# Seven-product feed-forward block: three of the seven products accumulate in PSUM onto three others, and the feature differences of the down projection are formed in the gate/up phase

## The chip, the cores and the metric

The kernel runs on one core of a Trainium2 chip, as one program. The metric is device time in microseconds (us), median of several executions. Beside the plain executions there is one profiled execution; every duration in this text comes from its trace. The engines are TensorE (PE, with its weight loads as PEld), VectorE (DVE), ScalarE (ACT), GpSimd (POOL) and SyncE (SP), which issues the transfers.

## The reference

A decoder trunk of two layers. Each layer mixes tokens in three ways (window attention, a state-space layer, latent attention), and then runs a gated feed-forward network, which is all that this change touches. Tokens: 1024. D_MODEL is 1024, D_FF is 2816.

```python
D_FF = ((8 * D_MODEL // 3 + 255) // 256) * 256
...
        h = rms_norm(x, ln2_g[l])
        x = x + (jax.nn.silu(h @ w_gate[l]) * (h @ w_up[l])) @ w_down[l]
    return rms_norm(x, final_g)
```

Everything is float32, so the kernel keeps about that precision: each operand of a matmul is split into a rounded part (hi) and the rest (lo), and three matmuls (hi by hi, hi by lo, lo by hi) stand for one.

## The kernel before

**Seven products for eight.** Activations lie with features on the partitions and tokens along the free axis, in two halves of 512 tokens (`HALF`). A feed-forward matmul is cut into 2 by 2 blocks of the weights and 2 by 2 of the activations (feature halves by token halves), and the four results are made of seven block products, as in Strassen's scheme, with Winograd's sums. The products are numbered 1 to 7. Each has a weight sum and an activation difference as operands, and the seven results are added into the four outputs, which the code calls (0,0), (0,1), (1,0), (1,1).

**One product.** `product` accumulates one product in one PSUM bank (tag `f`, 128 x 512 float32, 7 banks in the first layer and 8 in the second). For each slot of the contraction it issues three matmuls: L1621 (hi by hi), L1622 (hi weight, lo block), L1623 (lo weight, hi block). The weights come by DMA into `raw`; `halves` forms their sums `S` on DVE (L1563); `weight_block` and `split` make hi on ACT (cast, L242) and lo on POOL (L243) in tiles `wt`. The activation blocks are made by `combine` (a difference of two loaded tiles on DVE, L1606, in place) and `block` (hi by ACT, L1596; lo on DVE, L1597, or on POOL for products 5 and 7).

**Gate/up phase.** `ffn_begin` starts products 1 and 2 of the pairs 0 to 2 while the blocks of the other products are still being built; that stretch is called the head below. Then `ffn_pair` runs for the 11 pairs of 256 features. Each does seven products of four slots for gate and for up: 84 + 84 matmuls. `after` reads each finished product: ACT copies product 1, and DVE adds the others (L226) into the intermediate sums `u2`, `u3`, in tiles that are called B0 to B3, and into `gc`, `uc`. `finished` makes silu(gate) x up of one of the four results (tanh on ACT, then DVE at L235 and L226) and writes it to DRAM, into `actd`. A pair writes four results of 256 KB, 44 in a layer.

**Down stage.** `w_down` is walked in 15 windows: (d, p0, p1) is the output pair d with the feature pairs p0 to p1-1 as slots. A window runs the seven products over 2 to 4 slots. Where a window needs a feature pair for the first time, its four results are loaded from `actd` into B0 to B3, and its seven blocks are formed then, four of them by a difference. Eight windows bring pairs that are new (11 in all, hence 44 differences), seven bring none, the last among these. After each product DVE adds it, times one half, to one or two tiles of x (`TO`, at L235: x<-f,x), and products 1 and 6 also to a running sum `part` (tiles gs1, us1, gc, uc). In the windows without new pairs, but the last, product 5 goes by ACT (a copy `t`) and POOL (adds at L1839). The squares for the next norm are added on POOL (L1660).

**Order.** A scheduler orders the instructions of each engine from the program and its dependences. The order of the products is `ORDER` = 1, 2, 5, 6, 7, 3, 4, and `LAST` in the last window.

Of the kernel before, what the change touches and what calls it, by code (L numbers as in the profile page):

```python
# [22 lines left out]
HALF = 512  # L23
# [28 lines left out]
ORDER = (1, 2, 5, 6, 7, 3, 4)  # L52
LAST = (1, 2, 6, 7, 4, 5, 3)
BLOCKS = [[(b, k) for k in SLOTS for b in LAST[:2]], [(b, k) for k in SLOTS for b in LAST[2:]]]
BLOCKS[1:] = BLOCKS[1][:16], BLOCKS[1][16:]
TO = {1: ((0, 0),), 2: ((0, 0),), 5: ((0, 1), (1, 1)), 6: (), 7: ((1, 0), (1, 1)), 3: ((0, 1),), 4: ((1, 0),)}
# [3 lines left out]


# [154 lines left out]
class Trunk:  # L216
# [129 lines left out]
    def setup(self):  # L346
# [24 lines left out]
        self.actd = self.dp.tile([FT, 2, 128, HALF], F32, "actd")  # L371
# [1246 lines left out]
    def product(self, p, w, xs):  # L1618
        n = len(xs)
        for i, (k, (xh, xl)) in enumerate(xs):  # L1620
            self.T.matmul(p, w[0][:, k, :], xh, start=(i == 0), stop=False)  # L1621
            self.T.matmul(p, w[0][:, k, :], xl, start=False, stop=False)  # L1622
            self.last = self.T.matmul(p, w[1][:, k, :], xh, start=False, stop=(i == n - 1))  # L1623

    def after(self, b, p, tag, r):

        def new(n):
            if n[0] == "u":
                return self.ld.tile([128, HALF], F32, f"B{2 * int(n[1]) - 4 + (tag == 'u')}", 1)
            return self.fw.tile([128, HALF], F32, tag + n, 1)  # L1630
# [70 lines left out]
    def ffn_begin(self, l, pair, places):  # L1701
# [216 lines left out]
```

## Time and profile before

| what | us |
|---|---|
| median of three executions | 2389.26 (2388.66 to 2393.57) |
| profiled execution | 2391.46 |
| its span in the trace | 2389.5 |
| layer 0: head, gate/up, down | 101.1, 365.0, 254.5 |
| layer 1: head, gate/up, down | 100.1, 347.0, 254.5 |

The six stretches are 1422.2 us of the span. They were cut by hand at 503.9, 605, 970, 1224.5 in layer 0 and at 1669.9, 1770, 2117, 2371.5 in layer 1, where the first matmul of the head, the first of the steady pairs, the first of the down stage and its last stand. In layer 0 the gate/up stretch also holds tables for the next layer's state-space part, hence its greater length. Outside these stretches nothing is changed.

### The profile page before, as it was taken

What the parts mean: (1) busy time and instruction counts of PE and PEld (TensorE: products, weight loads), DVE (VectorE), ACT (ScalarE), POOL (GpSimd) and SP (SyncE); (2) the same over time, 40 slices, a digit from 0 to 9 for tenths busy, and PEclk for the clock granted to TensorE, in tenths of its full rate; (3) what the DMA queues carried; (4) which work ended last, traced back from release to release, by engine and by line L of the source; (5) the groups of instructions that cost most, each with busy time, mean ns of one, the idle gap of its engine ahead of it and who ended that gap; (6) DMA issues with size and microseconds to landing.
All of it is one profiled execution on the core that took longest, in us unless ns stands there. A gap on an engine that the chain in (4) does not pass through costs nothing. (4 is left out here: it accounts for less than half of the span.)

```text
span 2389.5 us, 31562 instructions
## 1 busy us (share of the span) xinstructions
PE 2233.2 (93%) x10460; PEld 1797.1 (75%) x10460; DVE 1754.5 (73%) x3079; ACT 996.6 (42%) x1992; POOL 1223.5 (51%) x1066
## 2 busy tenths in 40 slices
PE   7999889998999999899889998899899999999997
PEld 5688667876778878677668887687678888877776
DVE  7676975569876665998974578656886465689997
ACT  5254664543233333443333456544333333344334
POOL 1363653145565555677663354531555555557765
PEclk9899889998999999999989999899999999999999
DMA  6623343533332342432233232545252223243312
GB/s 214 178 77 74 100 115 127 178 100 88 117 109 84 97 129 79 127 112 88 81 119 81 65 107 65 153 127 155 88 165 88 85 74 93 67 128 101 108 60 81
DMA packets 263931, 255.85 MB, mean 107 GB/s; under 512 B 41450, under 2 KB 207193, under 8 KB 263769
## 3 DMA queue, kind: packets, MB, share of 16 engines
q1 hardware_dynamic: 263768, 253.84, 35.3%
q8 instruction: 83, 1.36, 0.2%
q14 instruction: 80, 0.65, 0.1%
HBM read 181.56 MB, written 65.92 MB: 104 GB/s over the span
## 5 line engine op out<-in xcount | busy, mean ns | idle before, releaser
L1621 PE MATMUL f<-b,wt 128*128 128x512 f32 x1848 | 740.8, 402 | 40.1 <-ACT wt L242 29.7
L1623 PE MATMUL f<-b,wt 128*128 128x512 f32 x1848 | 736.6, 402 | 21.3 <-POOL wt L243 20.5
L1622 PE MATMUL f<-b,wt 128*128 128x512 f32 x1848 | 736.6, 400 | 7.8 <-DVE b L1597 7.7
L243 POOL TENSOR_TENSOR wt<-raw,wt 128x512 fp32r<-128x512 f32 (+3 forms) x332 | 496.4, 1501 | 472.7 <-ACT wt L242 350.9
L1621 PEld LDWEIGHTS f<-b,wt 128*128 128x128 f32 x1848 | 354.3, 192 | 136.7 <-ACT wt L242 45.7
L1623 PEld LDWEIGHTS f<-b,wt 128*128 128x128 f32 x1848 | 354.4, 192 | 120.2 <-POOL wt L243 41.9
L243 POOL TENSOR_TENSOR wt<-S,wt 128x512 fp32r<-128x512 f32 (+2 forms) x222 | 300.5, 1355 | 272.9 <-ACT wt L242 269.6
L1622 PEld LDWEIGHTS f<-b,wt 128*128 128x128 f32 x1848 | 353.8, 191 | 91.3 <-DVE b L1597 13.7
L242 ACT CAST wt<-raw 128x512 fp32r<-128x512 f32 (+3 forms) x356 | 227.7, 646 | 305.4 <-PE f L1623 150.4
L242 ACT CAST wt<-S 128x512 fp32r<-128x512 f32 (+2 forms) x222 | 126.9, 573 | 247.6 <-DVE S L1563 158.6
L235 DVE SCALAR_TENSOR_TENSOR x<-f,x 128x512 f32<-128x512 f32 x216 | 141.6, 679 | 1.4 <-DVE x L235 0.5
L1596 ACT CAST b<-B 128x512 fp32r<-128x512 f32 x140 | 84.6, 618 | 136.6 <-DVE B L1606 83.7
L266 PE MATMUL mm<-b,wt 128*128 128x512 f32 x320 | 131.8, 412 | 7.3 <-DVE x L235 6.2
L267 PE MATMUL mm<-b,wt 128*128 128x512 f32 x320 | 128.2, 401 | 0.7 <-DVE b L235 0.7
L268 PE MATMUL mm<-b,wt 128*128 128x512 f32 x320 | 127.9, 400 | 0.0
L226 DVE TENSOR_TENSOR B<-B,f 128x512 f32<-128x512 f32 x176 | 119.2, 679 | 7.7 <-PE f L1623 4.1
L243 DVE TENSOR_TENSOR tl<-pt,th 128x512 fp32r<-128x512 f32 (+2 forms) x176 | 96.4, 553 | 38.2 <-ACT th L242 35.4
L1563 DVE TENSOR_TENSOR S<-raw,raw 128x512 f32<-128x512 f32 (+2 forms) x74 | 61.7, 836 | 72.5 <-DMA raw<-in_w_gate 38.2
L242 ACT CAST th<-pt 128x512 fp32r<-128x512 f32 (+2 forms) x176 | 82.9, 477 | 67.6 <-PE pt L1296 30.0
L1278 POOL TENSOR_SCALAR pr<-pr,den 128x128 f32<-128x128 f32 (+3 forms) x64 | 48.6, 763 | 120.4 <-DVE den L1277 117.5
L1597 DVE TENSOR_TENSOR b<-B,b 128x512 fp32r<-128x512 f32 x100 | 101.3, 1019 | 9.4 <-ACT b L1596 9.1
L1563 DVE TENSOR_TENSOR S<-raw,S 128x512 f32<-128x512 f32 (+2 forms) x74 | 69.5, 940 | 30.8 <-POOL wt L243 30.8
(440 smaller groups left out, 4152.8 us busy)
## 6 DMA issues: line engine op xcount, KB each, us to landing
raw<-in_w_gate SPq DMA_DIRECT2D x50, 512.0 KB, 3.8
raw<-in_w_up SPq DMA_DIRECT2D x50, 512.0 KB, 4.1
B<-actd SPq DMA_DIRECT2D x80, 256.0 KB, 2.9
raw<-in_w_out SPq DMA_DIRECT2D x32, 512.0 KB, 4.4
raw<-in_w_down SPq DMA_DIRECT2D x40, 384.0 KB, 3.2
x<-xe SPq DMA_DIRECT2D x48, 256.0 KB, 2.9
raw<-in_w_in SPq DMA_DIRECT2D x22, 512.0 KB, 4.4
actd<-gc SPq DMA_DIRECT2D x44, 256.0 KB, 2.1
```

Of the source, the lines that this page charges most:

```text
L226: self.V.tensor_tensor(out=out, in0=a, in1=b, op=op)
L235: self.V.scalar_tensor_tensor(out=out, in0=a, scalar=s, in1=b, op0=op0, op1=op1)
L242: self.A.copy(hi, src)
L243: (eng or self.V).tensor_tensor(out=lo, in0=src, in1=hi.bitcast(F32), op=ALU.subtract)
L266: self.T.matmul(ps, wh, xh, start=(i == 0), stop=False)
L267: self.T.matmul(ps, wh, xl, start=False, stop=False)
L268: self.T.matmul(ps, wl, xh, start=False, stop=(i == n - 1))
L1563: tt = lambda o, x, y, op: (self.G if b in self.gpre else self.V).tensor_tensor(out=o, in0=x, in1=y, op=op)
L1597: rest = lambda: (eng or self.V).tensor_tensor(out=t[1], in0=src, in1=t[0].bitcast(F32), op=ALU.subtract)
L1621: self.T.matmul(p, w[0][:, k, :], xh, start=(i == 0), stop=False)
L1622: self.T.matmul(p, w[0][:, k, :], xl, start=False, stop=False)
L1623: self.last = self.T.matmul(p, w[1][:, k, :], xh, start=False, stop=(i == n - 1))
```

## The change

Products 2, 3 and 4 no longer get a PSUM bank of their own. Product 2 is accumulated onto product 1, product 3 onto product 5, product 4 onto product 7, in the same bank, after the earlier one was read there. `ONTO` says which, `bank` hands out the bank, and the matmul starts without clearing it. The order becomes 1, 5, 2, 6, 7, 3, 4. So that the sums come out, the early products go to fewer outputs: `TO` lists five adds to x in a window where it listed eight. In the last window only product 2 is accumulated.

In the gate/up phase the (0,0) result is now finished straight from the two PSUM banks. All seven activation blocks of a pair (four of them differences) are formed there on DVE by `keep_blocks`, and all seven are written to `actd`, where four results were. In the down stage `stored` loads the seven, each into a tile of its own out of a rotation (x tiles, squares' tiles, B0 to B3), and `combine` is no longer called there. For the pairs 0 to 2 the (0,0) result is written in the head and loaded again.

```diff
-ORDER = (1, 2, 5, 6, 7, 3, 4)
-LAST = (1, 2, 6, 7, 4, 5, 3)
+ORDER = (1, 5, 2, 6, 7, 3, 4)
+ONTO = {2: 1, 3: 5, 4: 7}
+AHEAD, BUILT = (1, 2), (5, 6, 7, 3, 4)
+LAST = (1, 6, 2, 7, 4, 5, 3)
...
-TO = {1: ((0, 0),), 2: ((0, 0),), 5: ((0, 1), (1, 1)), 6: (), 7: ((1, 0), (1, 1)), 3: ((0, 1),), 4: ((1, 0),)}
+TO = {1: (), 2: ((0, 0),), 5: ((1, 1),), 6: (), 7: ((1, 1),), 3: ((0, 1),), 4: ((1, 0),)}
+TO_LAST = {**TO, 5: ((0, 1), (1, 1)), 7: ((1, 0), (1, 1))}
...
+        mm = lambda w, x, i: self.T.matmul(p, w, x, start=(i == 0 and not onto), stop=(i == 3 * n - 1), skip_group_check=onto)
...
         elif b == 2:
-            r[0, 0] = new("c")
-            self.tt(r[0, 0], r["s1"], p, ALU.add)
+            r[0, 0] = p
         elif b == 6:
-            r["u2"] = new("u2")
+            r["u2"], r[1, 1] = new("u2"), new("c")
             self.tt(r["u2"], r["s1"], p, ALU.add)
+            self.tt(r[1, 1], r["u2"], r[5], ALU.add)
         elif b == 7:
-            r["u3"], r[1, 1] = new("u3"), new("c")
-            self.tt(r["u3"], r["u2"], p, ALU.add)
-            self.tt(r["u2"], r["u2"], r[5], ALU.add)
-            self.tt(r[1, 1], r["u3"], r[5], ALU.add)
+            self.tt(r[1, 1], r[1, 1], p, ALU.add)
         elif b == 3:
-            self.tt(r["u2"], r["u2"], p, ALU.add)
-            r[0, 1] = r["u2"]
+            r[0, 1] = new("u3")
+            self.tt(r[0, 1], r["u2"], p, ALU.add)
         elif b == 4:
-            self.tt(r["u3"], r["u3"], p, ALU.add)
-            r[1, 0] = r["u3"]
+            r[1, 0] = r["u2"]
+            self.tt(r[1, 0], r["u2"], p, ALU.add)
+
+    def bank(self, b, r, ps, nf):
+
+        r[b] = r[ONTO[b]] if b in ONTO else ps.tile([128, HALF], F32, "f", nf)
+        return r[b]
...
+    def keep_blocks(self, pair, e, a):
+
+
+        def put(b, t):
+            self.dma(out=self.actd[pair, b], in_=t)
+        if e in ((0, 0), (1, 1)):
+            put(1 if e == (0, 0) else 3, a[e])
+        elif e == (0, 1):
+            self.tt(a[0, 0], a[0, 1], a[0, 0], ALU.subtract)
+            put(5, a[0, 0])
+            self.tt(a[0, 1], a[1, 1], a[0, 1], ALU.subtract)
+            put(7, a[0, 1])
+            self.tt(a[1, 1], a[1, 1], a[0, 0], ALU.subtract)
+            put(6, a[1, 1])
+        else:
+            put(2, a[1, 0])
+            self.tt(a[0, 0], a[1, 0], a[1, 1], ALU.subtract)
+            put(4, a[0, 0])
...
-            t = {}
-            for q in fresh:
-                t[q] = [self.ld.tile([128, HALF], F32, f"B{i}") if q else self.x_tile(i % 2, i // 2, False) for i in range(4)]
-                for i in range(4):
-                    self.dma(out=t[q][i], in_=self.actd[2 * q + i // 2, i % 2])
-            made = {}
+            def stored(b, q):
+
+                t = next(first if n < 2 else middle if n < ENDS else last)()
+                self.dma(out=t, in_=self.actd[q, b])
+                return self.block(b, q % 4, t, self.G if b in self.bsplit else None)
+            made, bank = {}, {}
...
-                p = ps.tile([128, HALF], F32, "f", nf)
-                self.product(p, next(ws), [(q - p0, self.blk[b][q % 4]) for q in range(p0, p1)])
+                onto = b in ONTO and not (end and b != 2)
+                p = bank[b] = bank[ONTO[b]] if onto else ps.tile([128, HALF], F32, "f", nf)
+                self.product(p, next(ws), [(q - p0, self.blk[b][q % 4]) for q in range(p0, p1)], onto)
...
-                for i, h in TO[b]:
+                for i, h in TO_LAST[b] if end else TO[b]:
```

The scheduler moves more than the diff shows. In the fences below, names are the program's, with buffer numbers. In layer 1's down stage, TensorE ran product 2 of window (3, 9, 11) right behind product 1, in a bank of its own (f_4852 after f_4848; the two wt tiles are their weights):

```order
L1621 MATMUL f_4848_21690<-b120_4813_21533,wt_4851_21695 128x512
L1622 MATMUL f_4848_21690<-b121_4814_21534,wt_4851_21695 128x512
L1623 MATMUL f_4848_21690<-b120_4813_21533,wt_4851_21695 128x512
L1621 MATMUL f_4852_21706<-b210_4801_21505,wt_4853_21707 128x512
L1622 MATMUL f_4852_21706<-b211_4802_21506,wt_4853_21707 128x512
L1623 MATMUL f_4852_21706<-b210_4801_21505,wt_4853_21707 128x512
```

In the changed kernel the same place reads as follows, from the last matmuls of product 4 of the window before (onto f_4673, that window's product 7) over products 6 (f_4690) and 7 (f_4692) of this one to product 2, which goes onto f_4681, where product 1 is.

```order
L1625 MATMUL f_4673_21438<-b421_4662_21372,wt_4676_21469 128x512
L1625 MATMUL f_4673_21438<-b420_4661_21371,wt_4676_21469 128x512
L1625 MATMUL f_4690_21534<-b620_4652_21353,wt_4691_21536 128x512
L1625 MATMUL f_4692_21547<-b710_4634_21317,wt_4693_21549 128x512
L1625 MATMUL f_4692_21547<-b711_4635_21318,wt_4693_21549 128x512
L1625 MATMUL f_4681_21494<-b210_4628_21305,wt_4689_21524 128x512
L1625 MATMUL f_4681_21494<-b211_4629_21306,wt_4689_21524 128x512
```

Between the end of product 1 and the start of product 2, and between 7 and 4, the order now holds some 20 matmuls of other products in the windows of two and three slots; product 4 of a window runs inside the window behind it.

On VectorE the down stage of before has, around window (1, 5, 8) of layer 1, the block differences (L1606), the lo parts (L1597), the adds of a product to x (L235) and to the running sum us1 (L226):

```order
L226 TENSOR_TENSOR us1_4462_19973<-us1_4462_19973,f_4585_20521 128x512
L235 SCALAR_TENSOR_TENSOR x2_0_4418_19871<-f_4585_20521,x2_0_4418_19871 128x512
L1597 TENSOR_TENSOR b211_4643_20782<-B2_4634_20752,b210_4642_20781 128x512
L1597 TENSOR_TENSOR b611_4652_20823<-B0_4632_20750,b610_4651_20822 128x512
L235 SCALAR_TENSOR_TENSOR x2_0_4418_19871<-f_4591_20544,x2_0_4418_19871 128x512
L1606 TENSOR_TENSOR B2_4634_20752<-B2_4634_20752,B0_4632_20750 128x512
L235 SCALAR_TENSOR_TENSOR x2_1_4419_19873<-f_4595_20563,x2_1_4419_19873 128x512
L235 SCALAR_TENSOR_TENSOR x3_1_4421_19877<-f_4595_20563,x3_1_4421_19877 128x512
```

The changed kernel has there, for the same window (products 1 and 2 in f_4556, product 6 in f_4565; f_4552 is products 7 and 4 of a window before):

```order
L230 TENSOR_TENSOR us1_4304_19831<-us1_4304_19831,f_4556_20933 128x512
L1601 TENSOR_TENSOR b401_4619_21275<-B0_4617_21272,b400_4618_21274 128x512
L239 SCALAR_TENSOR_TENSOR x1_0_4377_20175<-f_4552_20882,x1_0_4377_20175 128x512
L1567 TENSOR_TENSOR S_4597_21176<-raw_4590_21152,raw_4591_21154 128x384
L239 SCALAR_TENSOR_TENSOR x2_0_4254_19725<-f_4556_20933,x2_0_4254_19725 128x512
L230 TENSOR_TENSOR us1_4304_19831<-us1_4304_19831,f_4565_20982 128x512
L1567 TENSOR_TENSOR S_4576_21058<-S_4576_21058,raw_4572_21040 128x384
```

The differences are gone and each bank of two products has one add to x at its end. Counted over a whole layer, the adds x<-f,x go from 108 to 71, the 44 differences of the down stage to none (40 of them on B tiles), POOL's adds at L1839 from 12 to 6, and the 44 differences come back in the gate/up phase. The end of a pair there had adds of a product's bank and the finishing of a result, as here:

```order
L226 TENSOR_TENSOR B0_4203_18569<-B0_4203_18569,f_4216_18639 128x512
L235 SCALAR_TENSOR_TENSOR B0_4203_18569<-t_4220_18675,B0_4203_18569 128x512
L226 TENSOR_TENSOR B1_4206_18588<-B1_4206_18588,f_4218_18657 128x512
L226 TENSOR_TENSOR B0_4203_18569<-B0_4203_18569,B1_4206_18588 128x512
L226 TENSOR_TENSOR B2_4209_18607<-B2_4209_18607,f_4221_18680 128x512
```

DVE's order now has at such a place:

```order
L230 TENSOR_TENSOR B2_4165_19088<-gc_4154_19007,B2_4165_19088 128x512
L239 SCALAR_TENSOR_TENSOR B0_4153_19006<-t_4171_19150,B0_4153_19006 128x512
L230 TENSOR_TENSOR gc_4154_19007<-gc_4154_19007,gc_4149_18983 128x512
L230 TENSOR_TENSOR B1_4157_19027<-B1_4157_19027,f_4161_19049 128x512
L230 TENSOR_TENSOR B0_4153_19006<-B0_4153_19006,B1_4157_19027 128x512
L230 TENSOR_TENSOR gc_4149_18983<-B0_4153_19006,gc_4154_19007 128x512
```

Three of these rows (the first, third and last) are differences. In exchange a full pair has ten adds of a PSUM bank where it had fourteen, since product 2 needs none and products 6 and 7 need fewer. SP issues 77 writes to `actd` in a layer where it issued 44, and 77 loads from it (and 3 more in the gate/up phase) where it issued 44.

## Rows read from the trace of the kernel before

**Rows 1.** The page: busy time and share of the span, by engine.

```profile
PE 2233.2 (93%) x10460; PEld 1797.1 (75%) x10460; DVE 1754.5 (73%) x3079; ACT 996.6 (42%) x1992; POOL 1223.5 (51%) x1066
```

**Rows 2.** Busy time by stretch: head, gate/up, down of layer 0, then of layer 1.

```profile
core 0: us, PE busy (x) PEld busy (x) DVE busy (x) ACT busy (x) POOL busy (x), PEclk, DMA share, GB/s
503.90:605.00 101.10, 88.47 (x362) 68.22 (x361) 88.14 (x111) 36.68 (x63) 58.06 (x38) 0.92 0.30 91
605.00:970.00 365.00, 361.63 (x1597) 291.91 (x1596) 255.92 (x359) 115.56 (x203) 198.73 (x154) 0.99 0.33 102
970.00:1224.50 254.50, 230.75 (x926) 175.26 (x924) 235.13 (x297) 106.67 (x209) 186.54 (x143) 0.97 0.36 107
1669.90:1770.00 100.10, 88.92 (x363) 68.20 (x361) 83.72 (x104) 36.52 (x63) 58.21 (x38) 0.91 0.39 122
1770.00:2117.00 347.00, 347.00 (x1512) 283.73 (x1511) 216.47 (x291) 111.20 (x188) 181.41 (x130) 1.00 0.28 87
2117.00:2371.50 254.50, 232.95 (x929) 177.40 (x927) 228.14 (x297) 106.42 (x209) 180.44 (x140) 0.95 0.28 84
```

**Rows 3.** Waits of TensorE in layer 1's down stage: us, times, longest.

```profile
PE f L1621 <- ACT wt L242: 10.6, 11, 1.9
PE f L1623 <- POOL wt L243: 7.4, 10, 1.5
```

**Rows 4.** Waits of ScalarE in the same stretch.

```profile
ACT wt L242 <- DVE S L1563: 58.9, 22, 7.5
ACT b L1596 <- DVE B L1606: 42.4, 19, 5.8
ACT b L1596 <- DMA B<-actd: 26.2, 15, 3.9
```

**Rows 5.** Busy time in four short stretches of it; columns as in group 2.

```profile
2117.00:2132.20 15.20, 12.53 (x45) 8.82 (x44) 11.35 (x16) 6.66 (x15) 7.89 (x7) 0.89 0.58 189
2203.70:2221.70 18.00, 14.92 (x43) 9.80 (x42) 17.40 (x23) 8.17 (x17) 11.94 (x11) 0.72 0.46 131
...
2319.80:2334.20 14.40, 11.64 (x44) 7.27 (x43) 11.99 (x20) 7.32 (x16) 7.63 (x9) 1.00 0.10 30
2334.20:2357.00 22.80, 18.55 (x65) 13.75 (x64) 15.21 (x18) 8.16 (x17) 22.24 (x18) 0.85 0.06 18
```

**Rows 6.** VectorE by line and shape, same stage: busy us, mean ns, idle before.

```profile
L235 DVE SCALAR_TENSOR_TENSOR x<-f,x 128x512 f32<-128x512 f32 x107 | 70.1, 679 | 0.6
L1597 DVE TENSOR_TENSOR b<-B,b 128x512 fp32r<-128x512 f32 x50 | 50.1, 1009 | 5.4 <-ACT b L1596 5.3
L1606 DVE TENSOR_TENSOR B<-B,B 128x512 f32<-128x512 f32 x40 | 43.2, 1080 | 1.7 <-POOL b L1597 1.6
```

**Rows 7.** PE at line L1623 alone, 2117.05 to 2187.70 us; then VectorE's timeline.

```profile
2117.05:2187.70 70.65, 33.24 (x85) 16.57 (x84) 0.95 0.36 112
...
2199.14 0.68 DVE L226 TENSOR_TENSOR us<-us,f 128x512 f32<-128x512 f32 x1
```

**Rows 8.** POOL by line, layer 1's down stage.

```profile
L1839 POOL TENSOR_TENSOR x<-x,t 128x512 f32<-128x512 f32 x12 | 17.9, 1513 | 0.0
```

**Rows 9.** VectorE in layer 1's gate/up phase, by line, then one of its waits.

```profile
L226 DVE TENSOR_TENSOR B<-B,f 128x512 f32<-128x512 f32 x69 | 46.9, 680 | 0.4
L226 DVE TENSOR_TENSOR B<-B,B 128x512 f32<-128x512 f32 x17 | 18.2, 1072 | 0.3
...
DVE B L226 <- PE f L1623: 60.2, 16, 6.9
```

**Rows 10.** VectorE in layer 1's head (1669.9 to 1737 us), by line.

```profile
L226 DVE TENSOR_TENSOR gc<-gc,uc 128x512 f32<-128x512 f32 x3 | 5.1, 1690 | 0.1
L235 DVE SCALAR_TENSOR_TENSOR gc<-acc,gc 128x512 f32<-128x512 f32 x3 | 3.5, 1183 | 0.0
```

**Rows 11.** DMA issues on SP's queue: count, KB each, us from issue to landing.

```profile
B<-actd SPq DMA_DIRECT2D x80, 256.0 KB, 2.9
...
actd<-gc SPq DMA_DIRECT2D x44, 256.0 KB, 2.1
```

More of the change, by code (lines that the diff above doesn't have):

```diff
@@ L59 @@
            (2, 5, 8), (3, 6, 9), (0, 8, 11), (3, 9, 11), (1, 8, 11), (2, 8, 11)]
+ENDS = next(i for i, (d, a, b) in enumerate(WINDOWS) if b == WINDOWS[-1][2])
 def _bits12(v):
@@ L370, in setup @@
         self.xe = self.dp.tile([2, KT, 128, HALF], F32, "xe")
-        self.actd = self.dp.tile([FT, 2, 128, HALF], F32, "actd")
+        self.actd = self.dp.tile([FT // 2, 8, 128, HALF], F32, "actd")
         self.zd = [self.dp.tile([128, 8, 128], F32, f"zd{i}") for i in range(2)]
@@ L1629, in new @@
                 return self.ld.tile([128, HALF], F32, f"B{2 * int(n[1]) - 4 + (tag == 'u')}", 1)
-            return self.fw.tile([128, HALF], F32, tag + n, 1)
+            return self.fw.tile([128, HALF], F32, tag + n, 1 + (tag + n == "gc"))
         r[b] = p
@@ L1713, in ffn_begin, with finished @@
         self.begun[pair] = r
-        for b in ORDER[:2]:
+        for b in AHEAD:
             for m in range(2):
-                p = self.fps.tile([128, HALF], F32, "f", self.nf)
+                p = self.bank(b, r[m], self.fps, self.nf)
                 w = self.weight_block(b, raw[m][:, 4 * b - 4:4 * b])
-                self.product(p, w, [(k, self.blk[b][k]) for k in SLOTS])
+                self.product(p, w, [(k, self.blk[b][k]) for k in SLOTS], b in ONTO)
                 yield
                 self.after(b, p, "gu"[m], r[m])
-        self.finished(pair, (0, 0), r, self.sqp.tile([128, HALF], F32, "acc1", 1))
-    def finished(self, pair, e, r, t=None):
+        t = self.sqp.tile([128, HALF], F32, "acc1", 1)
+        self.finished(pair, (0, 0), r, t, t)
+        self.dma(out=self.actd[pair, 1], in_=t)
+    def finished(self, pair, e, r, t=None, out=None):
         g, u = r[0][e], r[1][e]
         t = self.fw.tile([128, HALF], F32, "t", 1) if t is None else t
+        out = g if out is None else out
         self.act(t, g, AF.Tanh, scale=0.5)
-        self.stt(g, t, 1.0, g, ALU.add, ALU.mult)
-        self.tt(g, g, u, ALU.mult)
-        self.dma(out=self.actd[2 * pair + e[0], e[1]], in_=g)
+        self.stt(out, t, 1.0, g, ALU.add, ALU.mult)
+        self.tt(out, out, u, ALU.mult)
+        return out
     def ffn_pair(self, l, pair):
@@ L1737, in ffn_pair @@
         r = self.begun.pop(pair, None)
-        order = ORDER[2:] if r else ORDER
+        order = BUILT if r else ORDER
+        a = {}
+        new = lambda: self.fw.tile([128, HALF], F32, "gc", 2)
+        if r:
+            a[0, 0] = new()
+            self.dma(out=a[0, 0], in_=self.actd[pair, 1])
         r = r or [{}, {}]
@@ L1742, in ffn_pair @@
             for m in range(2):
-                p = self.fps.tile([128, HALF], F32, "f", self.nf)
-                self.product(p, next(ws[m]), [(k, self.blk[b][k]) for k in SLOTS])
+                p = self.bank(b, r[m], self.fps, self.nf)
+                self.product(p, next(ws[m]), [(k, self.blk[b][k]) for k in SLOTS], b in ONTO)
                 yield
@@ L1747, in ffn_pair @@
             for e in DONE.get(b, ()):
-                self.finished(pair, e, r)
+                a[e] = self.finished(pair, e, r, None, new() if e == (0, 0) else None)
+                self.keep_blocks(pair, e, a)
+    def keep_blocks(self, pair, e, a):
[14 more added lines that the diff above has]
+            put(4, a[0, 0])
     def ffn(self, l, tp, side, other):
@@ L1774, in ffn @@
             self.late = []
-            for b in ORDER[2:]:
+            for b in BUILT:
                 for k in SLOTS:
@@ L1795, in ffn @@
         part = {}
+        spare = [lambda i=i: self.ld.tile([128, HALF], F32, f"B{i}", 1) for i in range(4)]
+        early = [lambda i=i: self.x_tile(i % 2, i // 2, False) for i in range(4)]
+        early += [lambda: self.sqp.tile([128, HALF], F32, "sq", 3)] * 3
+        early += [lambda h=h: self.sqp.tile([128, HALF], F32, f"acc{h}", 1) for h in range(2)]
+        first, middle, last = (itertools.cycle(x) for x in (early, early[4:] + spare, spare))
         def add(dst, src):
@@ L1820, in ffn @@
                     for b in ORDER:
[L1821 removed]
+                        made[b, q] = stored(b, q)
             for b in order:
```

15 lines of the change are left out of this document (7 added, 8 removed).

## The prediction

> **What bounds the kernel now.** I began with the page: TensorE is busy 93% of the span, VectorE 73% [rows 1]. That is an average over stages, so the next view is the table by stretch [rows 2]. In layer 1's gate/up phase PE is busy 347.00 of 347.00 us with 1512 matmuls, 229.5 ns each, at a granted clock of 1.00: nothing can be won there unless matmuls go, and the change takes none away. The two down stages have 926 and 929 matmuls in 254.5 us. At 229.5 ns they would take 212.5 and 213.2, so 42.0 and 41.3 us are time in which PE was kept waiting or was slowed. The heads have 362 and 363 matmuls in 101.1 and 100.1 us, 83.1 and 83.3 at that pace: 18.0 and 16.8 over. The most that any change to this block can win with the same matmuls is therefore 83.3 + 34.8 = 118 us.
>
> What keeps PE waiting in the down stage? By the waits it is weight tiles, the hi part from ACT (10.6 us) and the lo part from POOL (7.4) [rows 3]. Followed one step back, ACT itself waits 58.9 us for the weight sums S of VectorE, 42.4 us for the block differences at L1606, and 26.2 us for loads [rows 4]. So VectorE is late, and its busy time says why: 235.13 and 228.14 us, more than the 213 that PE needs [rows 2]. In the two gate/up phases VectorE is busy 255.92 of 365 and 216.47 of 347, 70% and 62%, and there 1597 and 1512 matmuls run at 228.6 and 229.5 ns: no excess at either share.
>
> The excess isn't spread evenly. Four short stretches hold 5.1 + 8.1 + 4.3 + 7.9 = 25.4 of layer 1's 41.3 us (length less PEld's count times 0.2295: 15.2 - 10.1, 18.0 - 9.9, 14.4 - 9.9 and so on, rounded) [rows 5]. In the second VectorE is busy 17.40 of 18.0 and the granted clock is 0.72. In the last POOL is busy 22.24 of 22.8: it, not VectorE, is the bound there.
>
> **The change, part by part.** *Adds to x.* 37 of 108 go per layer. One takes 0.679 us [rows 6]: 25.1 us less on VectorE.
>
> *Differences in the down stage.* 44 go per layer, 40 of them on B tiles at 1.080 us [rows 6]; I take these 40, 43.2 us, and leave the four on x tiles out. VectorE then has 235.1 - 68.3 = 166.8 and 228.1 - 68.3 = 159.8 us, 78 and 75% of PE's 213. It is no longer the bound of the stage.
>
> *POOL.* Six of twelve adds at L1839 go, 1.513 us each [rows 8]: 9.1 us of 186.5 and 180.4, so some 177 and 171 remain, 83 and 80% of 213. POOL is next.
>
> *ACT.* It makes as many copies and casts as before. Its 42.4 us of waits for differences fall away; the blocks wait for a load instead.
>
> *Transfers.* 77 loads from actd in a layer for 44, and 77 writes for 44, of 256 KB. A load landed 2.9 us after its issue, a write 2.1 us [rows 11]. The DMA share in the stages is 0.28 to 0.36 [rows 2]; loads that grow by 33 x 256 KB = 8.4 MB, over the 84 GB/s of 254.5 us = 21.4 MB, make about 0.39. The bounds are nothing (they are issued ahead into nine or more tiles) and, if each of the 33 more held up the blocks behind it by its 2.9 us, 96 us. I take nothing for the steady windows, because ACT's waits for loads cost PE little even now (26.2 us on ACT beside PE's waits for blocks too small to be among the rows), and keep a part of the high end in the third case below.
>
> *Gate/up phase.* A full pair gets four differences, two SBUF operands each, 1.072 us by the nearest row, and loses four adds of a bank, 0.680 us [rows 9]: 4.3 - 2.7 = 1.6 us more a pair, 13 us in eight pairs. VectorE had 216.5 of 347 and waits 60.2 us for PE there [rows 9], so PE does not notice: zero. Without that cover it would cost 13 us a layer. The two rows differ in one operand, a bank or a second SBUF tile. [...] The sum itself takes POOL's durations as they are.
>
> *The head.* The adds that make (0,0) go: six at about 0.68 us. gc<-gc,uc (5.1 us for three) and gc<-acc,gc (3.5) become operations on a bank, six at 0.68 [rows 9, 10]: 4.1 + 8.6 - 4.1 = 8.6 us a layer less on VectorE, which builds the blocks that PE waits for. The bounds of the gain are 0 and 8.6, since part of the excess is in ACT and weights; I take half, 4. A new wait: product 2 starts one product (12 matmuls, 2.8 us) after product 1's end and ACT must have copied it by then. Nothing in the rows prices it; it lies before the blocks are complete, and the half that I give away covers it.
>
> *Shared banks.* In a window of the down stage product 2 waits until product 1 has been read by VectorE, and 4 until 7 was. The order puts some 20 matmuls between, 20 x 0.2295 = 4.6 us. How late does VectorE read now? By 2187.70 us PE had loaded 84 weights of line L1623, 7 x (2 + 3 + 3 + 4), the first four windows. The fifth window's product 1 is the next 9 matmuls, about 2.1 us, so it ended near 2190.0; us<-us,f, which reads it, began at 2199.14 [rows 7]. That is 9 us, twice the slack. But VectorE was then over 90% busy; at 75 to 78% its queue should be short. Lower bound: no wait. Upper bound: 9.1 - 4.6 = 4.5 us in each of 28 waits a layer, 126 us. I take 3 us a layer, near the low end, since the nearest rows at such a load, the gate/up phases, show PE without excess, though reads there trail too. What would wait with it: matmuls of the other products queued behind on PE, then ACT and POOL for free weight tiles. On the other side, a window now holds four banks for seven, which lets PE run further ahead; I give that nothing.
>
> **The sum.** Of some 41.7 us of excess in a down stage, the POOL-bound stretch (7.9) keeps 6, as one of its adds (1.5) goes. Of the other 34, a share remains that I scale by VectorE's load: none at 70% (the gate/up phase), all at 109% (mean of 235.1 / 212.5 and 228.1 / 213.2), and 76.5% lies at (76.5 - 70) / 39 = 17%; I take a quarter, 8 us, for the starts of windows, which wait on transfers. With 3 for the banks 17 remain and 24.7 go, 49 us in two layers. With 4 us from each head it is 57 us. The profiled execution took 2391.5 us; 2391.5 - 57 = 2334.5. The median of the runs lies 2.2 below the profiled one, so the forecast is **2332 us**.
>
> **The rivals.** *First (forecast), 0.60:* as above; its own range is 2310 to 2358, that is, 11 us more or 13 us less won in each layer than I took.
>
> *Second, 0.17: PE runs through.* VectorE's release also frees POOL and ACT, and only 6 us of a down stage remain: 35.7 x 2 = 71, with the whole 8.6 us of both heads 88 us: 2391.5 - 88 - 2.2 = 2301. For it: the waits of ACT on VectorE (58.9 and 42.4) are far the largest in the stage. Against: POOL at 80% and more.
>
> *Third, 0.13: weights or transfers take over.* POOL's lo parts already make PE wait 7.4 us [rows 3], and it stays at 80 to 83%; 33 more loads stand in SP's queue among the weights' own. If three quarters of the excess stays under a new name, some 10 us a layer go and the head gives nothing: 2391.5 - 20 - 2.2 = 2369. For it: the last of the short stretches is POOL's already [rows 5].
>
> *Fourth, 0.10: slower, by the shared banks.* The reads stay as late as they are, because VectorE's queue is in a fixed order and holds lo parts that wait for blocks (5.3 us of such idle time, [rows 6]) ahead of a bank's read. With 28 waits a layer, the whole excess of 42 us is eaten at 42 / 28 = 1.5 us a wait, a lag of 6.1 us; beyond that the kernel is slower. At 2 us it is 56 us a layer against 42 won: 28 us more in both, 2389.3 + 28 - 8 = 2409. The 9 us of today speak for it, the fall of VectorE's load against it. [...]
>
> **How the numbers follow.** About 0.2%, 4.8 us, is what a measurement of this kernel can tell from no change. The range 2294 to 2378 holds the first case whole, about two thirds of the second and most of the third, some 8 in 10; above it lies the fourth. The first two and most of the third are faster: 0.86. The third's weak end, with a few small bank waits on top, gives no change: 0.04. Slower: 0.10.
>
> **What would show each step.** Right: the two down stages fall from 254.5 to about 230 us; VectorE there is near 160 to 167 us, with about 71 adds x<-f,x; ACT's wait for differences is gone; the last short stretch is still POOL's; gate/up phases stay within 2 us of 365 and 347; the heads lose about 4 us. Wrong: a line of PE waiting for VectorE's x or us, gs, gc at the start of a product, of over 40 us a layer (fourth case); PE waiting for POOL's wt or ACT's b behind loads, over 20 us a layer (third); a gate/up phase over 350 us in layer 1, which would mean that the differences there are not hidden; a head longer than before, which would be the copy of product 1.

## The result, and the profile after

| what | before | after |
|---|---|---|
| median, us | 2389.32 (2388.66 to 2393.57, 4 runs) | 2332.28 (2330.30 to 2337.12, 4 runs) |
| ratio | | 0.9761 (95%: 0.974 to 0.9781) |
| profiled execution's span | 2389.5 | 2328.6 |

The forecast of 2332 us was met, 57 us less than before. The terms behind it were not met one by one, so the result is worth taking apart. First the table by stretch of the changed kernel, in the order of [rows 2] and with the same columns (head, gate/up, down, of layer 0 and then of layer 1):

```profile
498.50:601.00 102.50, 86.94 (x362) 68.02 (x360) 89.32 (x112) 36.51 (x63) 57.16 (x38) 0.95 0.37 110
601.00:968.20 367.20, 363.01 (x1596) 292.44 (x1597) 269.96 (x352) 118.82 (x212) 205.55 (x155) 0.99 0.41 131
968.20:1190.20 222.00, 216.86 (x926) 173.75 (x926) 175.34 (x221) 102.97 (x196) 167.75 (x135) 0.99 0.44 139
1634.90:1734.70 99.80, 86.92 (x362) 68.22 (x361) 83.20 (x100) 36.41 (x63) 57.81 (x38) 0.95 0.45 143
1734.70:2086.30 351.60, 349.10 (x1513) 285.04 (x1512) 234.03 (x286) 114.34 (x196) 188.90 (x131) 1.00 0.36 116
2086.30:2310.80 224.50, 218.85 (x928) 176.18 (x926) 174.16 (x224) 105.81 (x200) 161.49 (x132) 0.98 0.38 120
```

The down stages lost 32.5 and 30.0 us, 62.5 together, where 49 were forecast. The heads changed by +1.4 and -0.3 where 8 were to be won, and the gate/up phases got longer by 2.2 and 4.6 where nothing was to change. In all that is 54.6 us (1422.2 down to 1367.6). The rest of the span's 60.9 lies outside these stretches, most of it ahead of the first head, which begins at 498.5 us for 503.9. TensorE's order up to there isn't quite that of before, since the scheduler moved some projections. But of the kernels below, five with before's order (it among them) begin the head at 500.1 to 506.0 us and nine with the order of the change at 498.5 to 509.8, so those 5 us are spread, not gain. The medians lie 57.0 us apart, 3.9 less than the two profiled spans.

The waits of TensorE in layer 1's down stage, answering to [rows 3], hold the new kind, a product waiting for the reader of the bank that it goes onto (the first two lines; us and x are the readers' outputs):

```profile
PE f L1625 <- ACT us L1874: 2.1, 1, 2.1
PE f L1625 <- DVE x L239: 2.0, 1, 2.0
PE f L1625 <- POOL wt L247: 1.3, 2, 0.9
PE f L1625 <- ACT wt L246: 0.3, 1, 0.3
```

They are 5.7 us where the two lines of [rows 3] held 18.0. ScalarE's waits in the same stretch, answering to [rows 4]:

```profile
ACT wt L246 <- PE f L1625: 37.6, 36, 3.1
ACT wt L246 <- DVE S L1567: 37.1, 18, 3.3
...
ACT b L1600 <- DMA acc<-actd: 4.4, 2, 2.4
ACT b L1600 <- DMA sq<-actd: 4.3, 4, 1.4
```

The 42.4 us for block differences are gone, and first comes a wait for TensorE: ACT is ahead and waits for weight tiles that PE still reads. For about as long (37.1 us) it waits for VectorE's weight sums. PE is now what holds ACT up in much of the stage.

To see where in the stage the time went, I cut it by count of matmuls into a start (the first 84), a middle (672) and an end (168). At 229.5 ns, the pace of the prediction, they need 19.3, 154.2 and 38.6 us. Layer 1 of the changed kernel, columns as above:

```profile
2086.30:2112.60 26.30, 22.95 (x86) 17.25 (x85) 25.64 (x36) 13.56 (x27) 18.58 (x14) 0.87 0.81 268
2112.60:2267.50 154.90, 154.90 (x674) 126.22 (x673) 114.05 (x147) 68.64 (x129) 110.23 (x93) 1.00 0.40 123
2267.50:2310.80 43.30, 41.00 (x172) 32.70 (x170) 34.48 (x42) 23.61 (x44) 32.68 (x26) 0.96 0.06 19
```

And the kernel before, cut the same way:

```profile
2117.10:2143.80 26.70, 22.79 (x85) 16.30 (x84) 22.84 (x33) 11.84 (x24) 13.71 (x11) 0.94 0.44 135
2143.80:2319.80 176.00, 165.37 (x674) 128.08 (x673) 164.22 (x207) 70.48 (x139) 129.43 (x99) 0.96 0.32 96
2319.80:2371.50 51.70, 44.69 (x172) 32.95 (x170) 40.97 (x58) 24.08 (x46) 37.30 (x32) 0.93 0.05 16
```

The middle went from 176.0 to 154.9 us, all that could be won there; the end from 51.7 to 43.3; the start hardly at all. Of the middle's 21.1 us, 10.6 were idle time of TensorE (176.00 less 165.37 busy). The other 10.5 are the same 674 matmuls done in 154.90 us of busy time for 165.37: before, the granted clock stood at 0.5 for 13.7 us of the middle (0.96 over the whole of it), and after it never did there (1.00). In the start, where 7.0 us over PE's need are left (26.3 - 19.3; 7.4 before), VectorE is busy 25.64 of 26.30 us.

### The profile page after: what moved, and what is told of

It reads as the page before. It is cut to its first block, busy times and chain, and to the rows that moved or that the text cites. A ratio compares the mean times of both kernels' runs of the same rounds, so it can differ in the third digit from the quotient of the medians.

```text
span 2328.6 us, 31600 instructions
## 1 busy us (share of the span) xinstructions
PE 2201.8 (95%) x10460; PEld 1792.4 (77%) x10460; DVE 1671.7 (72%) x2917; ACT 1000.7 (43%) x1992; POOL 1200.8 (52%) x1054
## 5 line engine op out<-in xcount | busy, mean ns | idle before, releaser
L1625 PE MATMUL f<-b,wt 128*128 128x512 f32 x5544 | 1310.0, 397 | 43.2 <-ACT wt L246 10.3
L1625 PEld LDWEIGHTS f<-b,wt 128*128 128x128 f32 x5544 | 1049.9, 190 | 295.7 <-POOL wt L247 16.8
L247 POOL TENSOR_TENSOR wt<-S,wt 128x512 fp32r<-128x512 f32 (+2 forms) x222 | 293.0, 1323 | 235.4 <-ACT wt L246 228.8
L247 DVE TENSOR_TENSOR tl<-pt,th 128x512 fp32r<-128x512 f32 (+2 forms) x176 | 96.3, 551 | 44.3 <-ACT th L246 41.6
L239 DVE SCALAR_TENSOR_TENSOR x<-f,x 128x512 f32<-128x512 f32 x142 | 94.9, 680 | 27.4 <-PE f L1625 27.1
L894 POOL TENSOR_SCALAR pr<-pr,den 128x256 f32<-128x256 f32 (+1 forms) x128 | 70.2, 562 | 23.7 <-DVE den L892 20.0
L879 POOL COPY sb<-nsink 128x2 f32<-128x2 f32 x64 | 18.7, 294 | 117.7 <-ACT pr L242 115.4
L1273 PE MATMUL sc<-k,q 96*128 96x512 f32 (+7 forms) x288 | 73.9, 381 | 4.4 <-ACT pr L242 3.3
L242 ACT ACTIVATE pr<-sb,nm 128x257 f32<-128x257 f32 (+1 forms) x128 | 62.6, 492 | 34.8 <-DVE nm L886 34.4
L271 PEld LDWEIGHTS mm<-b,wt 128*128 128x128 f32 x320 | 62.1, 194 | 15.9 <-DVE b L239 4.4
L272 PEld LDWEIGHTS mm<-b,wt 128*128 128x128 f32 x320 | 61.9, 193 | 16.1 <-DVE wt L247 2.9
L1600 ACT CAST b<-x 128x512 fp32r<-128x512 f32 x78 | 47.7, 620 | 61.0 <-DVE x L1610 52.0
```

The costliest lines, as they stand in the source:

```text
L239: self.V.scalar_tensor_tensor(out=out, in0=a, scalar=s, in1=b, op0=op0, op1=op1)
L242: self.A.activation(out=out, in_=a, func=func, **kw)
L247: (eng or self.V).tensor_tensor(out=lo, in0=src, in1=hi.bitcast(F32), op=ALU.subtract)
L271: self.T.matmul(ps, wh, xl, start=False, stop=False)
L272: self.T.matmul(ps, wl, xh, start=False, stop=(i == n - 1))
L894: self.G.tensor_scalar(out=pr[:, j, lo_k:256], in0=pr[:, j, lo_k:256], scalar1=den[:, j:j + 1], scalar2=0.0, op0=ALU.mult, op1=ALU.add)
```

## The experiments

**One part at a time.** Four kernels: the order alone, the accumulation alone, the moved differences alone, and the changed kernel without the accumulation in its down stage.

The order alone (in the head, products 1 and 2 still go ahead):

```diff
-ORDER = (1, 2, 5, 6, 7, 3, 4)
+ORDER = (1, 5, 2, 6, 7, 3, 4)
```

> The kernel before with the product order 1, 5, 2, 6, 7, 3, 4 and nothing else; every product keeps its own bank. Load theory (VectorE's work bounds the down stage): the same work in another order, so 2389 us within 5, down stages still near 254 us each. Order theory (the order alone frees PE): most of the 57 us, 2345 us or less.

Measured: ratio 1.0027 (1.0006 to 1.0048), 2399.17 us beside 2394.09. The order alone wins nothing; if anything it costs 0.3%.

The accumulation alone (from the changed kernel; the gate/up phase stores four results again):

```diff
-                self.keep_blocks(pair, e, a)
+                self.dma(out=self.actd[2 * pair + e[0], e[1]], in_=a[e])
...
-                        made[b, q] = stored(b, q)
+                        made[b, q] = self.combine(b, q % 4, t[q])
```

> Accumulation alone: the changed kernel with four results stored and the 44 differences of a layer formed in the down stage as before. Load theory: VectorE there loses only the adds (25 us) and stays near 99% of PE's 213 us, so about a quarter to a third of the excess goes, 10 to 13 us a layer: 2360 to 2372 us. Bank theory (four banks for seven let PE run ahead, and POOL's and VectorE's adds were what held it): 2345 us or less, within 15 us of the changed kernel.

Measured: 0.9947 (0.993 to 0.9964), 2382.26 us. Layer 1's down stage, start, middle and end:

```profile
2102.80:2135.60 32.80, 24.43 (x86) 16.82 (x84) 23.29 (x30) 12.57 (x24) 16.53 (x13) 0.84 0.38 119
2135.60:2310.70 175.10, 160.51 (x673) 125.96 (x672) 154.56 (x190) 71.30 (x140) 125.37 (x95) 0.99 0.31 95
2310.70:2355.00 44.30, 41.28 (x172) 32.67 (x170) 35.59 (x43) 23.58 (x44) 33.23 (x27) 0.96 0.06 18
```

The end has nearly all of its gain; the middle has none of it; the start is 6 us longer than before. Less was won than either theory had said, and of the profiled execution's gain the two down stages hold only 2.9 and 2.2 us: layer 0's gate/up phase gives 5.7 (359.6 for 365.3).

The moved differences alone (from the kernel before: `keep_blocks` and `stored` as in the change, with its order, banks and adds):

```diff
-                self.finished(pair, e, r)
+                a[e] = self.finished(pair, e, r)
+                self.keep_blocks(pair, e, a)
...
-                        made[b, q] = self.combine(b, q % 4, t[q])
+                        made[b, q] = stored(b, q)
```

> Moved differences alone: the kernel before, with its order, banks and adds, but seven blocks stored in the gate/up phase and loaded in the down stage. Load theory: VectorE in a down stage falls by 43 us to about 190 (90% of PE's 213), half of the excess goes, 15 to 20 us a layer: 2350 to 2362 us. Bank theory: 2375 us or more. If transfers were a cost (33 more loads a layer), PE would show waits behind loads, and the time would not fall.

Measured: 0.9939 (0.9916 to 0.9961), 2376.65 us. The same cut:

```profile
2116.70:2151.20 34.50, 24.05 (x86) 16.76 (x85) 29.35 (x49) 14.71 (x30) 20.79 (x16) 0.90 0.66 219
2151.20:2306.00 154.80, 154.80 (x674) 126.18 (x673) 122.77 (x165) 63.63 (x127) 111.80 (x94) 1.00 0.40 122
2306.00:2354.80 48.80, 42.59 (x172) 32.05 (x170) 39.84 (x56) 24.08 (x46) 37.09 (x30) 0.97 0.06 17
```

The whole gain of the middle is there, 21.2 us, with all 108 adds to x and a bank for each product. But the start is 7.8 us longer and layer 0's gate/up phase 11.5 us (376.8 for 365.3; both cut at the same matmul): there the differences are not hidden as long as the phase has its old fourteen adds. In layer 1 it grew by 4.0 (351.3 for 347.3), as much as in the changed kernel. In the stage as a whole VectorE was busy 192 us, 90% of PE's 213; in the middle it was busy 122.77 us, 80% of the 154.2 that PE needs, and there was no excess.

The changed kernel, down stage with own banks:

```diff
-                onto = b in ONTO and not (end and b != 2)
-                p = bank[b] = bank[ONTO[b]] if onto else ps.tile([128, HALF], F32, "f", nf)
+                onto = False
+                p = ps.tile([128, HALF], F32, "f", nf)
```

(with eight adds to x a window, as before).

> The changed kernel with the accumulation undone in the down stage only: seven banks a window, eight adds to x for five, order 1, 5, 2, 6, 7, 3, 4. Load theory: as e3 in the down stages, 2350 to 2362 us; VectorE near 190 us there. Bank-wait theory (sharing costs waits that are paid out of the gain): not slower than the changed kernel's 2332 by more than 10 us.

Measured: 0.9833 (0.9801 to 0.9865), 2352.81 us; start, middle and end of 25.5, 157.6 and 44.8 us. Its middle:

```profile
2123.40:2281.00 157.60, 156.79 (x674) 127.14 (x673) 133.47 (x179) 66.47 (x132) 118.09 (x98) 0.99 0.41 126
```

So the accumulation in the down stage, with the three adds a window that it saves, is a gain of some 0.7% by the medians in place of a cost. The stages show less: 6.1 and 3.4 us, 0.4%; the other 6 us between the profiled executions lie ahead of the first head (505.2 for 498.5 us), where the two kernels are the same. The whole change is more than its parts: two that alone gave 0.5 and 0.6% gave 2.4% together. Alone, each lengthened the start of the stage by 6 to 8 us; together they don't. In e2 PE waits there once 7.2 us for a block's hi part, in e3 10.5 us for weights (5.8 for hi parts, 4.7 for lo parts); why both go when the parts are joined no run settles.

**Which work of VectorE counts?** In the prediction its load was the measure. Three kernels are meant to change the load and the kind of work apart. First, 42.8 us of adds in each layer taken off the kernel before:

```diff
-                for i, h in TO[b]:
+                for i, h in () if b in (1, 5, 7) else TO[b]:
                     add(self.xT[2 * d + i][h], p)
```

> The kernel before with 63 of the 108 adds to x per layer left out in the down stage (those of products 1, 5 and 7 that VectorE does), which takes 42.8 us of work off VectorE there, as much as the 40 differences; part of the result is not computed. The differences stay where they were. Load theory (what counts is VectorE's busy time): the middle windows run clean, down stages of 230 to 240 us. Chain theory (what counts is that a block has to wait for load, difference, cast and lo in turn, among VectorE's two-operand work): the down stages stay above 247 us.

Measured: 0.9896 (0.9861 to 0.9931), 2367.08 us. The middle of layer 1's down stage:

```profile
2139.70:2310.20 170.50, 161.52 (x673) 125.87 (x672) 144.38 (x164) 69.68 (x139) 130.06 (x100) 0.99 0.32 98
```

5.5 us less than before, where the differences, 38 us of work in the middle, had given 21. The work by lines there, the adds and the differences of before and then the adds of e6:

```profile
L235 DVE SCALAR_TENSOR_TENSOR x<-f,x 128x512 f32<-128x512 f32 x73 | 48.0, 678 | 0.2
L1606 DVE TENSOR_TENSOR B<-B,B 128x512 f32<-128x512 f32 x34 | 38.2, 1124 | 1.7 <-POOL b L1597 1.6
```

```profile
L235 DVE SCALAR_TENSOR_TENSOR x<-f,x 128x512 f32<-128x512 f32 x30 | 20.3, 678 | 0.0
```

In the middle e6 took off 27.7 us of adds and no more, and VectorE stayed busy 144.38 us where e3 has 122.77, so the two weren't compared at the same load. The down stages, 246.4 and 243.7 us, lie between the ranges of both theories. The second kernel puts subtractions back that no block waits for:

```diff
                 self.dma(out=t, in_=self.actd[q, b])
+                if b in (4, 5, 6, 7):
+                    self.tt(self.fw.tile([128, HALF], F32, "t", 1), t, t, ALU.subtract)
```

> The kernel e3_diffs (seven stored blocks, own banks, old order) with 44 more VectorE subtractions per layer in its down stage, of the same shape and with two SBUF operands, whose result nobody uses. VectorE has again its 235 us of work there, but no block waits for a difference. Load theory: the down stages go back to 250 us or more. Chain theory: they stay at 238 to 243 us.

Measured: 1.0106 (1.0063 to 1.015), 2414.82 us. The middle:

```profile
2161.10:2340.20 179.10, 163.48 (x674) 126.75 (x674) 167.30 (x214) 69.31 (x137) 134.33 (x100) 0.98 0.42 130
```

24.3 us more than e3. So the chain theory falls: the work costs as much when nothing depends on it. The down stages, 256.2 and 253.6 us, are what the load theory had said. What speaks for the kind of work is POOL. Its groups in the middle, first before, then e3, then e7 (lo parts of 384 columns of weights, and of blocks; count, busy us, mean ns):

```profile
L243 POOL TENSOR_TENSOR wt<-raw,wt 128x384 fp32r<-128x384 f32 x29 | 36.2, 1256 | 5.1 <-ACT wt L242 5.1
...
L1597 POOL TENSOR_TENSOR b<-B,b 128x512 fp32r<-128x512 f32 x17 | 26.3, 1547 | 6.1 <-ACT b L1596 6.0
```

```profile
L244 POOL TENSOR_TENSOR wt<-raw,wt 128x384 fp32r<-128x384 f32 x27 | 30.9, 1150 | 5.9 <-ACT wt L243 5.9
...
L1598 POOL TENSOR_TENSOR b<-B,b 128x512 fp32r<-128x512 f32 x8 | 11.4, 1419 | 0.0
```

```profile
L244 POOL TENSOR_TENSOR wt<-raw,wt 128x384 fp32r<-128x384 f32 x29 | 36.6, 1269 | 3.3 <-ACT wt L243 3.3
...
L1598 POOL TENSOR_TENSOR b<-B,b 128x512 fp32r<-128x512 f32 x8 | 12.9, 1613 | 2.3 <-ACT b L1597 2.3
```

POOL's own operations get shorter when VectorE's subtractions go (1256 to 1150 ns) and longer when they come back (1269), though nobody touched them. In these three runs POOL's work is longer where VectorE has more operations with two SBUF tiles. The third kernel puts work of the other kind into e3, 44.8 us a layer for e7's 43.4 (44.2 in layer 0), but from a PSUM bank:

```diff
+                if fresh and b in (4, 5, 6, 7):
+                    for _ in range(len(fresh) * (2 if b in (4, 6) else 1)):
+                        self.stt(self.fw.tile([128, HALF], F32, "t", 1), p, 0.5, self.xT[2 * d][0], ALU.mult, ALU.add)
```

> The kernel e3_diffs with 66 more VectorE operations per layer in its down stage that read one PSUM bank and one x tile and whose result nobody uses: 66 x 0.68 = 45 us, as much VectorE time as the 44 spare subtractions of e7 took, but one SBUF operand each. [...] Load theory: 170 to 180 us, as e7.

Measured: 1.0051 (1.0034 to 1.0068), 2402.72 us. Its middle, and POOL's largest group there:

```profile
2171.00:2335.60 164.60, 159.10 (x674) 126.59 (x672) 148.39 (x217) 62.88 (x126) 110.55 (x93) 0.99 0.38 114
```

```profile
L244 POOL TENSOR_TENSOR wt<-raw,wt 128x384 fp32r<-128x384 f32 x26 | 29.7, 1152 | 4.9 <-ACT wt L243 4.8
```

9.8 us more than e3's 154.8, about half of the 15 to 25 that the load theory's 170 to 180 for the middle would add. POOL's operations kept their length (1152 ns for 1150), so it is not held up by such work, but VectorE's own queue still is late by it. Per microsecond of work in the middle: adds from PSUM moved it by 0.20 (e6: 5.5 us for 27.7) to 0.28 (e9: 9.8 for 35.3), subtractions of two SBUF tiles by 0.62 (e7: 24.3 for 39.0).

Outside the middle the contrast shrinks. The profiled spans of e7 and e9 are the same, 2406.9 us, 34.1 more than e3; the medians lie 0.5% apart, and the intervals of the ratios just overlap. In e9 19.4 of the 34.1 lie behind the down stages (9.5 between the layers, 9.9 behind the last matmul); that VectorE is late with its adds there is the author's estimate. So in the total these two kernels do not clearly show adds from PSUM to be the cheaper work.

Nor does the middle refute the load theory outright. By VectorE's busy time, which holds the lengthening beside POOL (1.15 us on average for 0.67 to 0.69 in before's stage, last section), layer 1's middles come out nearly in order: e3 122.8 us busy and 154.8 long, e4 133.5 and 157.6, e6 144.4 and 170.5, e9 148.4 and 164.6, e2 154.6 and 175.1, before 164.2 and 176.0, e7 167.3 and 179.1. An excess that sets in between e3 and e4 and then grows with the load would give most of that. It would not give that e9 is 5.9 us shorter than e6 with VectorE busier; there POOL is busy 110.6 us for 130.1. Another difference of e7 and e9 is untested: e7's operations stand in VectorE's queue ahead of a block's lo part, e9's behind a finished product.

**POOL's side.** Two edits of the kernel before take work off POOL and give it to VectorE:

```diff
-END_VIA = (5,)
+END_VIA = ()
```

> The kernel before with product 5 of the windows without new pairs added by VectorE from PSUM: POOL loses 12 adds of 1.5 us a layer, VectorE gets 12 of 0.68 us more. [...] Load theory (VectorE at 228 to 235 of 254 us is the bound): longer by up to 8 us a layer.

```diff
-START_POOL = (5, 7)
+START_POOL = ()
```

> The kernel before with the lo parts of the blocks of products 5 and 7 on VectorE too, where POOL made them: POOL loses some 20 operations of 1.55 us in a down stage and 8 in a head, VectorE gets as many of 0.7 to 1.1 us. [...] Load theory: VectorE goes from 230 to 245 us or more and the stage is longer by 10 to 20 us.

Measured: e10 0.9956 (0.9939 to 0.9973), 2381.23 us; e11 0.9905 (0.988 to 0.993), 2368.83 us. The middle of e10, then of e11:

```profile
2142.90:2314.90 172.00, 163.42 (x673) 126.58 (x673) 163.19 (x215) 68.83 (x135) 114.90 (x91) 0.97 0.33 99
```

```profile
2127.70:2300.20 172.50, 164.18 (x674) 127.66 (x672) 167.72 (x228) 72.12 (x140) 101.91 (x80) 0.97 0.32 97
```

In both the middle of layer 1 got shorter by some 4 us, with as much work for VectorE or more, so the sign is not that of VectorE's load; in e11 layer 0's middle did not move (175.0 for 175.2). As whole stages, layer 0 then layer 1, e10's are 7.2 and 8.9 us shorter than before, e11's 1.0 longer and 5.0 shorter. POOL has less work in both (114.90 and 101.91 us busy in the middle for 129.43). Whether that alone shortens the stage, or that there is less of it beside VectorE's, these two runs don't tell. e11's surprise is the head of layer 1:

```profile
1664.50:1752.70 88.20, 84.42 (x362) 67.78 (x361) 82.61 (x107) 35.95 (x63) 50.22 (x30) 0.96 0.43 134
```

88.2 us for 99.9 (cut at the same matmul), and 90.0 for 100.9 in layer 0, with VectorE about as busy as before (82.61 us for 83.72 in [rows 2]). With its eight lo parts on POOL the head is some 11 us longer.

**The small losses.** e5 exchanges the B tiles in every second pair:

```diff
-                return self.ld.tile([128, HALF], F32, f"B{2 * int(n[1]) - 4 + (tag == 'u')}", 1)
+                return self.ld.tile([128, HALF], F32, f"B{2 * ((int(n[1]) + odd) % 2) + (tag == 'u')}", 1)
```

> The changed kernel with the tiles B0, B1 and B2, B3 exchanged in every second pair of the gate/up phase, so that a pair's product 6 doesn't overwrite the tile whose write to DRAM was issued last. Theory (the 4.4 us that the gate/up phase of layer 1 lost are one wait of VectorE for that write, and TensorE's wait for the bank of product 5 behind it): layer 1's gate/up phase falls from 351.6 to 347 to 348 us, layer 0's by up to 4 us, in all 3 to 8 us off 2332. Rival (the wait comes from the load on VectorE): no change.

Measured: 0.9774 (0.9741 to 0.9807), 2332.12 us, in the total no gain over the change. Layer 1's gate/up phase fell from 351.6 to 349.2, about half of what was expected. The wait moved: VectorE had waited for B's write in the changed kernel,

```profile
PE f L1625 <- DVE gc L230: 2.5, 1, 2.5
...
DVE B L230 <- DMA actd<-B: 4.7, 1, 4.7
```

and in e5 it waits for the write of gc:

```profile
PE f L1625 <- DVE gc L230: 1.7, 1, 1.7
...
DVE gc L230 <- DMA actd<-gc: 4.4, 1, 4.4
```

e8 turns END_VIA off in the changed kernel, the same edit as in e10.

> The changed kernel with product 5 of the windows without new pairs added by VectorE from PSUM, not by ACT and POOL: six POOL adds of 1.5 us a layer go, six adds of 0.68 us come to VectorE. If POOL is what holds the last windows: 2 to 4 us a layer faster. If the remaining excess there is the order of reads: same within 3 us, or slower.

Measured: 0.9754 (0.9727 to 0.9782), 2330.76 us. Layer 1's down stage is 221.5 us for 224.5, layer 0's 222.5 for 222.0; in the total it can't be told from the change. The last kernel joins both with a third gc buffer:

```diff
-            return self.fw.tile([128, HALF], F32, tag + n, 1 + (tag + n == "gc"))
+            return self.fw.tile([128, HALF], F32, tag + n, 1 + 2 * (tag + n == "gc"))
```

> The changed kernel with e5's exchange of tiles, a third gc buffer (VectorE's wait had moved from the write of B to the write of gc), and e8's adds of product 5 on VectorE. If the two gains are real and add: gate/up phase of layer 1 at 347.5 us, down stages at 221 to 222, 2322 to 2328 us. If they were within the spread: 2330 to 2334 us.

Measured: 0.9744 (0.9717 to 0.977), 2329.75 us. Layer 1 is as expected, 347.3 us of gate/up and 220.9 of down stage. Layer 0's gate/up phase is 369.1 us, with PE waiting 7.1 us for VectorE's gc, more than in the changed kernel (3.9). In the total it is not clearly faster than the change.

## Why the prediction came out right, point by point

*The total* was right to within a microsecond, by errors of opposite sign: 13 us too little for the down stages, 16 too much for heads and gate/up phases (7.9 lost by the table, 8 won in the forecast), and 2 us that come from outside these stretches. That they cancel is luck. The 62.5 us of the down stages lie between the first case's 49 and the second's 71 (PE runs through), nearer to the second; in the middle of the stage PE does run through. A slip in the working changes nothing: by its own rule, PEld's counts, the four short stretches hold 5.1 + 8.4 + 4.5 + 8.1 = 26.1 us, not 25.4.

*Adds and differences.* The counts held. VectorE has 175 and 174 us of work there, where 167 and 160 were forecast, 8 and 14 too few: its other lines did not stay at their old sum. POOL has 168 and 161 where 177 and 171 were forecast: it lost 19 us a layer, only 9 of which are the six adds. Of the other 10 a part is two operations that fell into other stretches, and the rest is shorter operations: in layer 1 the lo parts of 384 columns went from 1257 to 1183 ns (from raw) and from 1203 to 1144 (from S).

*The excess scaled by VectorE's load* is the step that failed. I kept 8 us for it and 6 for the POOL-bound stretch at the end; together with the banks' 3, 17 us a layer. Measured: 9.5 (222.0 - 212.5) and 11.3 (224.5 - 213.2). In layer 1's middle 0.7 us are left of 21.8; most of the rest is the stage's start, 7.0 us, which the change hardly touched. The scale was wrong in its shape: put to e3's middle, where VectorE has 80% of PE's need, it would have left a quarter, and nothing was left. And VectorE's load is not the only measure, since e9 is shorter than e6 with VectorE busier, and layer 1's middle is shorter in e10 and e11 than before with VectorE as busy. In each of these the one with less work on POOL is the shorter. That operations of VectorE and POOL lengthen each other is shown below (VectorE's from 0.68 to 1.15 us on average); how much of the 21 us is due to that, and how much to the load of both engines, is not. The sum took POOL's durations as they were, and they did not stay: its largest group in the middle took 1256 ns before, 1150 in e3 without the differences and 1269 in e7 with as many subtractions put back.

*The end.* 13.1 us over PE's need before (51.7 - 38.6), 4.7 after; 6 were to stay. The accumulation gives most of it, since e2 has 44.3.

*The banks.* 3 us a layer were taken; layer 1's rows show 4.1, one wait on ACT's copy of a window's first product 1 and one on an add to x, and layer 0 has 2.5 of the same two. That they didn't become the fourth case is seen in e4: with own banks, and the eight adds that go with them, the stage is 3.4 us longer (227.9 for 224.5), not shorter.

*The heads.* 4 us each were to be won and none were. e11 shows that POOL's lo parts are on the path there (without them there it took 88.2 us for 99.9 in layer 1 and 90.0 for 100.9 in layer 0). A new wait of PE for VectorE's gc (4.6 us in layer 0, 1.9 in layer 1), a line that the heads of before don't have, may have taken up what the adds gave; no run shows it.

*The gate/up phase.* In layer 1 it passed the 350 us that the prediction had named as a sign of being wrong. The cover of 60.2 us was there, and the 1.6 us a pair are hidden in the steady pairs. What I missed is the seam between pairs that were begun ahead: they start with product 5, so the next pair overwrites a tile whose write to DRAM has only just been issued, VectorE waits 4.7 us for it and PE 2.5 for the bank behind it. e5 and e12 show that by moving and then removing it in layer 1. In layer 0 the cover depends on the fewer adds: with the accumulation and its fewer adds alone (e2) the phase is 5.7 us shorter than before, with the differences alone (e3) 11.5 longer, with both some 2 longer. In layer 1 it doesn't: there e3 grew as much as the change.

## What to carry to other kernels

When an engine seems to be the bound by its busy share, ask which of its operations also slow its neighbour: here subtractions of two SBUF tiles on VectorE lengthened the middle of the stage by 0.62 us per microsecond and adds from PSUM by 0.2 to 0.3, and POOL's unchanged operations grew by 10% (1150 to 1269 ns). Then read the total as well, since work that spares one stretch can come back behind it: e7 and e9 ended with the same span. Parts of a change can be worth more together, so a part that gives little alone (0.5 and 0.6%) is not yet refuted. And a total that is met says little of its terms; cut the stage and compare each.

Left open: the lo parts of e11 moved in the changed kernel too, where the heads might give some 10 us each. It wasn't tried.

## What the runs showed of the hardware that was not expected

How operations of VectorE and POOL lengthen each other can be read off the head of layer 1 in the changed kernel. First VectorE's timeline (start, length, line, names, count), then POOL's:

```profile
1684.67 4.59 DVE L1610 TENSOR_TENSOR x<-x,x 128x512 f32<-128x512 f32 x3
1689.18 5.71 DVE L1601 TENSOR_TENSOR b<-x,b 128x512 fp32r<-128x512 f32 x4
...
1705.44 0.68 DVE L1601 TENSOR_TENSOR b<-x,b 128x512 fp32r<-128x512 f32 x1
1706.05 0.67 DVE L230 TENSOR_TENSOR uc<-B,f 128x512 f32<-128x512 f32 x1
```

```profile
1688.67 5.08 POOL L1601 TENSOR_TENSOR b<-x,b 128x512 fp32r<-128x512 f32 x3
...
1700.36 3.42 POOL L247 TENSOR_TENSOR wt<-raw,wt 128x512 fp32r<-128x512 f32 x2
1712.68 1.30 POOL L247 TENSOR_TENSOR wt<-S,wt 128x512 fp32r<-128x512 f32 x1 [8.90 <-ACT wt L246]
```

POOL's three operations take 5.08 us, 1.69 each. VectorE takes 5.71 us for four beside them: three at 1.69 and one at 0.68 would make 5.75. At 1705.44, with POOL idle, the same line takes 0.68 us, about as much as an add from PSUM; and the POOL operation at 1712.68, which starts with VectorE at no such work, takes 1.30. The 1.69 us are less than 0.68 and 1.30 together.

It shows over a whole stage too. In layer 1's down stage of the kernel before, the trace has 133 operations of VectorE on 128x512 that read a PSUM bank, and all of them took 0.67 to 0.69 us, whether POOL was at work (108) or not (25). Of its 113 with two SBUF tiles the 33 beside which POOL did nothing took 0.67 to 0.69 us too; the other 80 took 1.15 on average, from 0.68 up to 1.82. A mean such as 1.08 us [rows 6] is a mixture of the two and prices neither: in this stage the time of such an operation depended on what POOL did beside it.
